# The second MLP layer of a hybrid decoder layer: eight units by seven products, with two running sets of PSUM banks

## The chip, the cores and the metric

The kernel runs on one core of one Trainium2 chip. A core has five engines with queues of their own: PE (TensorE, the matmuls), DVE (VectorE), ACT (ScalarE), POOL (GpSimd) and SP (SyncE, which here issues the transfers). Data lies in HBM, in SBUF and, for what PE writes, in the eight banks of PSUM, each 128 rows of 512 fp32 numbers. The metric is the device time of one execution in microseconds (us); lower is better.

## The reference

One Hymba layer in fp32: 1024 positions of width 1024, an attention and a recurrence side by side, an output projection, and an MLP of width 4096.

```python
x = x + rmsnorm(mixed, mix_post_norm[layer])
h = rmsnorm(x, mlp_pre_norm[layer])
ff = jnp.square(jax.nn.relu(h @ w_ff1[layer])) @ w_ff2[layer]
x = x + rmsnorm(ff, mlp_post_norm[layer])
```

The change lies in the third line's second product (1024 x 4096 by 4096 x 1024) and in the fourth line. The norm divides a row by its root mean square and multiplies by a gain per column.

## The kernel before

**Precision.** Every fp32 operand is split into a high part (ACT copies it in a rounded format) and a low part (DVE subtracts), in `split_into` (L97, L98), and each product is three matmuls, high by high, high by low and low by high, in `three_pass` (L101 to L103) and in the first layer's `mm1` (L1489 to L1491). Names end in h or l accordingly: ah and al are the activations' parts, bh and bl the weights'.

**First layer.** The 4096 hidden columns are 16 pairs of 256. A pair (`ff1(q)`, q = 2 to 15; pairs 0 and 1 go together ahead of them) is computed by the seven products of the Strassen-Winograd scheme, each of 12 matmuls, and the results are combined, passed through the squared ReLU and summed into the seven left operands which the second layer's seven products need: `act_sums` on POOL, L1557 to L1560. `act_store` writes them to `act_dram`. Two pairs make one unit of 512 hidden columns of the second layer, so there are units 0 to 7. Pairs 0 and 1, unit 0, are only squared and stored as they are (`act_plain`, into `act_raw`).

**Second layer.** It is a sum over the eight units. Units 1 to 7 go by seven products each, in three groups, (1), (2, 3, 4) and (5, 6, 7). Within a group the order is product, then unit, so that a product of all the group's units adds up in the same four banks (one for each block of 128 rows), and is then collected:

```python
if g == 0:
    ...
    S.activation(acc_at(p, i), pm, AF.Copy)
elif g == NG - 1 and p == 4:
    V.tensor_tensor(out=acc_at(p, i), in0=acc_at(p, i), in1=pm, op=ALU.subtract)
else:
    V.tensor_tensor(out=acc_at(p, i), in0=pm, in1=acc_at(p, i), op=ALU.add)
```

There is one SBUF sum for each of the seven products. The four output quadrants are made of them by `fold_in` (L1916) in the last group and after. One product of one unit is 24 matmuls (4 row blocks, 2 halves of 128 hidden rows, 3 passes). Unit 0 is computed last, in full: for each of the eight row blocks of the output 24 matmuls into two banks `fe`, whose content is added to the quadrants (L2053); ACT squares the sums with a running total (L2054), POOL makes the row's factor (L2058, L2066, L2067), DVE multiplies by the gain (`norm_gain`, L2028) and adds the residual (`end_out`, L2023), and two transfers of 256 KB write the row block. The last block's second half is cut in two (L2044 to L2048), with DVE squaring one of them.

**What sets the order.** Nothing is scheduled by a planner: the engines run their instructions in the order in which the program is written. At unit-product n the program issues the load of the left operand of n + 3 (`a_load`, L1824), prepares the parts of n + 2 (`prep`), makes the weights' sum for n + 4 (`prep_sum`, `b_source`, L1849 and L1855, on DVE), loads weights as buffers come free (`b_pump`, L1830), then issues the matmuls and, where the product is complete, its collection. Work beside these has its place in the table `at_last` or in `start2`, which runs between the products of the first layer's last pair. SBUF buffers come from pools (`small`, `large`) and are handed on when `drop` was called; a buffer's next writer waits for its last reader.

Of the kernel before, what the change touches and what calls it, by code (L numbers as in the profile page):

```python
# [35 lines left out]
def hymba_layer(ctx, tc, x, w_in, w_out, w_ff1, w_ff2, g_pre, lb_logits, g_mix, g_post,  # L36
# [63 lines left out]
    def three_pass(dst, lhs, rhs, start, stop):  # L100
        TE.matmul(dst, lhs[0], rhs[0], start=start, stop=False)  # L101
        TE.matmul(dst, lhs[0], rhs[1], start=False, stop=False)  # L102
        TE.matmul(dst, lhs[1], rhs[0], start=False, stop=stop)  # L103
# [1320 lines left out]
    act_raw = dp.tile([P, 2, 2, 2, 512], F32, name="actr")  # L1424
    act_dram = {u: dp.tile([P, 7, 2, 512], F32, name=f"actd{u}") for u in range(1, NPAIR // 2)}
# [145 lines left out]
    def act_plain(q):  # L1571

        l = lay.pop(q)
        nc.sync.dma_start(out=act_raw[:, q, 0, 0], in_=l["E1"][:, 0])
        nc.sync.dma_start(out=act_raw[:, q, 0, 1], in_=l["X"][:, 0])
        nc.sync.dma_start(out=act_raw[:, q, 1], in_=l["E1"][:, 1:3])
        drop(l["E1"], l["X"])


# [224 lines left out]
    for q in range(2, NPAIR - 1):  # L1804
        ff1(q)

# [3 lines left out]
    GROUPS = ((1,), (2, 3, 4), (5, 6, 7))  # L1810
    NG = len(GROUPS)
    APLACE = {1: 0, 2: 1, 4: 2, 5: 3, 6: 4, 7: 5, 3: 6}
    ORDER = (1, 5, 7, 6, 2, 4, 3)
    LAST = (1, 5, 7, 6, 2, 3, 4)
    units = [(g, p, h) for g in range(NG) for p in (LAST if g == NG - 1 else ORDER) for h in range(len(GROUPS[g]))]
# [4 lines left out]
    def a_load(n):  # L1820
        if n < n_units:
            g, p, h = units[n]
            axraw[n] = small.get(f"ar{n}")
            nc.sync.dma_start(out=axraw[n], in_=act_dram[GROUPS[g][h]][:, APLACE[p]])  # L1824

# [8 lines left out]
    def b_pump(g):  # L1834

        spare = sum((g, h) not in tt for h in range((len(GROUPS[g]) + 1) // 2)) if g >= 0 else 0
        while b_queue and b_queue[0][0] <= g + 1 and len(large.free) > spare:
            b_load(*b_queue.pop(0))

# [3 lines left out]
    def b_source(g, p, h):  # L1843
# [4 lines left out]
        if p == 7:  # L1848
            V.tensor_tensor(out=b12, in0=b22, in1=b12, op=ALU.subtract)  # L1849
            return b12  # L1850
        if p == 5 and h % 2 == 0:
            tt[g, h // 2] = large.get(f"tt{g}{h}")
        t = tt[g, h // 2][:, 2 * (h % 2):2 * (h % 2) + 2]
        in0, in1 = {5: (b12, b11), 6: (b22, t), 4: (t, b21)}[p]
        V.tensor_tensor(out=t, in0=in0, in1=in1, op=ALU.subtract)  # L1855
        return t
# [3 lines left out]
    def prep_sum(n):  # L1860
        if n < n_units:
            g, p, h = units[n]
            bsrc[n] = b_source(g, p, h)
            if g == NG - 1 and p == 4:
                drop(braw.pop((g, h, 1)))

    def prep(n):
# [9 lines left out]
        order = LAST if g == NG - 1 else ORDER  # L1877
        done_p = order[:order.index(p) + 1]

        def now(*needs):  # L1880
            return p in needs and all(x in done_p for x in needs)

        if p == 4 and (h % 2 or h == len(GROUPS[g]) - 1):
            drop(tt[g, h // 2])
        if now(1, 5, 7):
            drop(braw.pop((g, h, 0)))
        if now(2, 3, 4, 6, 7) and g < NG - 1:
            drop(braw.pop((g, h, 1)))

    cur = []  # L1890

    def mm2(n, i, first, last):
        (ah, al), (bh, bl) = aop[n], bop[n]
        c = slice(i * P, (i + 1) * P)
        for j in range(2):
            three_pass(cur[i], (ah[:, j, c], al[:, j, c]), (bh[:, j], bl[:, j]), first and j == 0, last and j == 1)

    def acc_at(p, i):
        return acc[p][i // 2][:, i % 2]

    def collect(g, p, i):

        pm = cur[i]
        if g == 0:
            if i == 0:
                acc[p] = [small.get(f"acc{p}{j}") for j in range(2)]
            S.activation(acc_at(p, i), pm, AF.Copy)
        elif g == NG - 1 and p == 4:
            V.tensor_tensor(out=acc_at(p, i), in0=acc_at(p, i), in1=pm, op=ALU.subtract)
        else:  # L1910
            V.tensor_tensor(out=acc_at(p, i), in0=pm, in1=acc_at(p, i), op=ALU.add)  # L1911
        drop(pm)

    def fold_in(p, o, j, op=ALU.add):

        V.tensor_tensor(out=acc[p][j], in0=acc[o][j], in1=acc[p][j], op=op)  # L1916


    def start2(p):
# [5 lines left out]
        elif p == 5:  # L1925
            drop(*bops["T1"])
            prep(0)
            prep_sum(2)
        elif p == 6:
# [4 lines left out]
            prep_sum(3)  # L1934
        elif p == 4:
            drop(*bops["T4"])
        elif p == 7:
            drop(*bops["T3"])
            prep(2)
# [18 lines left out]
    def plain_load(kind, q):  # L1958
        t = praw[kind, q] = large.get(f"{kind}p{q}")
        if kind == "w":  # L1960
            src = w_ff2[2 * q * P:(2 * q + 2) * P].rearrange("(j p) c -> p j c", j=2)
        else:
            src = act_raw[:, q].rearrange("p j a c -> p j (a c)")
        nc.sync.dma_start(out=t.rearrange("p (j a) c -> p j (a c)", j=2), in_=src)

    def plain_split(kind, q, j):
        if j == 0:
            plain[kind, q] = [large.get(f"{kind}p{x}{q}", F32R) for x in "hl"]
        hi, lo = (x[:, 2 * j:2 * j + 2] for x in plain[kind, q])
        split_into(hi, lo, praw[kind, q][:, 2 * j:2 * j + 2])  # L1970
        if j == 1:
            drop(praw.pop((kind, q)))

    def plain_op(kind, q, j, c0, n):
        return tuple(x.rearrange("p (j a) c -> p j (a c)", j=2)[:, j, c0:c0 + n] for x in plain[kind, q])

    n_last = n_units - 7 * len(GROUPS[-1])
# [162 lines left out]
```

## Time and profile before

| | us |
|---|---|
| median of 3 runs | 1231.04 (1230.53 to 1233.12) |
| the profiled execution | 1229.69 |
| its span in the trace | 1227.9 |
| busy: PE / DVE / ACT / POOL | 1206.1 / 840.0 / 538.8 / 289.7 |
| granted TensorE clock, mean | 0.997 of full speed |
| second layer, first matmul to the end of the span | 910.08 to 1227.9 |

The span is what the profile covers; the profiled execution took 1.79 us more than it. Rows of the trace give the start and duration of an instruction, its line, engine and operation, the tile that it writes and those that it reads, their shapes, and in brackets the idle time before it with the work that ended the wait. In groups, xcount is followed by the busy time in us, the mean of one in ns, and the idle time before them with its releasers.

### The profile page before, as it was taken

Reading aid. Unit: us, or ns where it says so; the run is one execution under the profiler, and the core shown is the slowest. Engines: PE = TensorE matmul, PEld = TensorE weight load, DVE = VectorE, ACT = ScalarE, POOL = GpSimd, SP = SyncE. Lnnn points to the kernel's source line nnn. Section 1 sums busy time; section 2 is a strip of 40 time slices with the busy share of each in tenths; the row PEclk is TensorE's granted clock in tenths of the full one; section 3 lists DMA queues with packets and bytes.
Section 4 is the critical chain, followed back from the end, with each engine's and each line's share of the span. In section 5 each row is a group of like instructions: output and inputs, shape, how many; then the busy total and the mean of one; then the engine's idle time right before and its main releaser. Section 6 shows DMA issues by size and latency. Waiting matters only on the chain. (4 is left out here: it accounts for less than half of the span.)

```text
span 1227.9 us, 16736 instructions
## 1 busy us (share of the span) xinstructions
PE 1206.1 (98%) x6264; PEld 1026.4 (84%) x6264; DVE 840.0 (68%) x1329; ACT 538.8 (44%) x1058; POOL 289.7 (24%) x253
## 2 busy tenths in 40 slices
PE   8999999999999999999999999999999999999997
PEld 8898989888788887778888888888878888888886
DVE  5584858575565657665589566666675866698966
ACT  7633333332566567844664222222247434344312
POOL 0000000032303130154230786565530000000012
PEclk9999999999999999999999999999999999999999
DMA  5221312123443455353424554353668444434423
GB/s 215 66 73 52 87 52 70 35 69 104 107 113 100 115 144 180 103 174 121 173 76 154 181 180 151 133 189 129 222 262 315 145 153 137 154 104 132 176 70 120
DMA packets 80417, 163.77 MB, mean 133 GB/s; under 512 B 23632, under 2 KB 30544, under 8 KB 80080
## 3 DMA queue, kind: packets, MB, share of 16 engines
q1 hardware_dynamic: 80336, 162.70, 40.5%
q8 instruction: 49, 0.80, 0.3%
q14 instruction: 32, 0.26, 0.1%
HBM read 112.16 MB, written 46.19 MB: 129 GB/s over the span
## 5 line engine op out<-in xcount | busy, mean ns | idle before, releaser
L101 PE MATMUL f<-bh,ah 128*128 128x512 f32 x392 | 152.5, 389 | 0.0
L102 PE MATMUL f<-bl,ah 128*128 128x512 f32 x392 | 152.5, 389 | 0.0
L103 PE MATMUL f<-bh,al 128*128 128x512 f32 x392 | 152.5, 389 | 0.0
L98 DVE TENSOR_TENSOR al<-ar,ah 128x1024 fp32r<-128x1024 f32 x49 | 60.6, 1237 | 48.2 <-ACT ah L97 17.7
L101 PEld LDWEIGHTS f<-bh,ah 128*128 128x128 f32 x392 | 73.6, 188 | 15.4
L102 PEld LDWEIGHTS f<-bl,ah 128*128 128x128 f32 x392 | 73.6, 188 | 15.2
L103 PEld LDWEIGHTS f<-bh,al 128*128 128x128 f32 x392 | 73.6, 188 | 15.2
L97 ACT ACTIVATE ah<-ar 128x1024 fp32r<-128x1024 f32 x49 | 52.2, 1065 | 51.1 <-PE f L103 25.4
L2058 POOL TENSOR_SCALAR fp<-fss 128x1 f32<-128x1 f32 x8 | 3.7, 459 | 269.5 <-ACT fd L2054 269.5
L862 DVE TENSOR_TENSOR pt<-pt,pt 128x512 fp32r<-128x512 f32 (+1 forms) x56 | 34.9, 630 | 34.1 <-ACT pt L861 33.9
L1557 POOL TENSOR_TENSOR e<-x,e 128x512 f32<-128x512 f32 x14 | 20.6, 1475 | 135.8 <-DVE x L1508 135.8
L93 POOL TENSOR_SCALAR ms<-hss 128x8 f32<-128x8 f32 x4 | 1.0, 258 | 214.9 <-ACT ysq L600 214.9
L821 ACT ACTIVATE prob<-prob,unm 128x128 f32<-128x128 f32 (+2 forms) x96 | 48.5, 508 | 4.7 <-DVE unm L815 4.3
L97 ACT ACTIVATE bh<-br 128x1024 fp32r<-128x1024 f32 x28 | 29.9, 1066 | 42.9 <-PE f L103 37.6
L663 POOL TENSOR_TENSOR ql<-qf,q 64x512 fp32r<-64x512 f32 x16 | 21.5, 1346 | 97.3 <-ACT q L662 96.7
L861 ACT ACTIVATE pt<-pt 128x512 fp32r<-128x512 f32 (+1 forms) x56 | 30.3, 549 | 24.0 <-PE pt L858 23.6
L1911 DVE TENSOR_TENSOR acc<-f,acc 128x512 f32<-128x512 f32 x52 | 33.8, 685 | 8.2 <-PE f L103 8.2
L97 ACT ACTIVATE bh<-tt 128x1024 fp32r<-128x1024 f32 x21 | 22.3, 1061 | 38.2 <-PE f L103 25.9
L763 DVE CUSTOM_DVE_ANT_0 prob<-ps,tab 128x256 f32<-128x256 f32 (+3 forms) x56 | 26.5, 502 | 17.3 <-PE ps L760 11.0
L98 DVE TENSOR_TENSOR bl<-br,bh 128x1024 fp32r<-128x1024 f32 x28 | 34.2, 1221 | 2.9 <-PE f L102 2.5
L98 DVE TENSOR_TENSOR wl<-raw,wh 128x1024 fp32r<-128x1024 f32 x21 | 26.9, 1279 | 9.5 <-ACT wh L97 9.1
L879 PE MATMUL pov<-pt,v 128*128 128x512 f32 (+3 forms) x144 | 30.4, 320 | 0.3 <-DVE pt L862 0.2
(1650 smaller groups left out, 3806.4 us busy)
## 6 DMA issues: line engine op xcount, KB each, us to landing
ar<-actd SPq DMA_DIRECT2D x49, 512.0 KB, 3.7
raw<-in_w_in_dram SPq DMA_DIRECT2D x28, 512.0 KB, 3.6
w1r<-in_w_ff_dram SPq DMA_DIRECT2D x14, 1024.0 KB, 6.4
br<-in_w_ff_dram SPq DMA_DIRECT2D x14, 1024.0 KB, 8.0
actd<-e SPq DMA_DIRECT2D x17, 768.0 KB, 4.3
actd<-e SPq DMA_DIRECT2D x11, 1024.0 KB, 4.1
xr<-in_x_dram SPq DMA_DIRECT2D x8, 512.0 KB, 9.7
raw<-in_w_out_dram SPq DMA_DIRECT2D x8, 512.0 KB, 3.9
```

The lines of the kernel that those rows point to most:

```text
L97: S.activation(hi, src, AF.Copy)
L98: eng.tensor_tensor(out=lo, in0=src, in1=f32(hi), op=ALU.subtract)
L101: TE.matmul(dst, lhs[0], rhs[0], start=start, stop=False)
L102: TE.matmul(dst, lhs[0], rhs[1], start=False, stop=False)
L103: TE.matmul(dst, lhs[1], rhs[0], start=False, stop=stop)
L663: G.tensor_tensor(out=lo[a:b], in0=full[a:b], in1=f32(stacks[i]["q"][a:b, sl]), op=ALU.subtract)
L763: V.tensor_tensor_reduce(out=out, in0=pS, in1=tab, scale=1.0, scalar=-3.0e38, op0=ALU.add, op1=ALU.max, accum_out=acc)
L821: S.activation(pe, pe, AF.Exp, bias=r["nm"][:, j:j + 1], accum_out=r["dn"][:, j:j + 1])
L861: S.activation(hi, ptv, AF.Copy)
L862: V.tensor_tensor(out=lo, in0=ptv, in1=f32(hi), op=ALU.subtract)
L879: TE.matmul(o, v.rearrange("p a d -> p (a d)"), x[q], start=g == 0 and q == 0, stop=g == 2 + hf and n == len(ops) - 1 and q == 1, skip_gro ...
L1911: V.tensor_tensor(out=acc_at(p, i), in0=pm, in1=acc_at(p, i), op=ALU.add)
```

## The change

Unit 0 joins the others. The groups are (0, 1), (2, 3, 4) and (5, 6, 7), all by seven products: 56 unit-products in place of 49 and the plain unit. For that, unit 0's left operands are made as well: `act_plain` stores the four plain pieces of pairs 0 and 1, `act_again` reads a pair's 1 MB back after pairs 5 and 8 of the first layer, `act_rest` makes the three sums with four operations on DVE ahead of pairs 7 and 10, and stores them.

The seven SBUF sums become four, one for each quadrant (C11, C12, C21, C22), and what several quadrants share is added up in PSUM. Three sets of banks take turns. Set x holds products 1 and 2: product 1 is copied by ACT to set y, and product 2 is then added onto it in x, which gives C11. On y, products 6, 7 and 4 are added one after another, and what is there is collected after each: for C12, C22 and C21. Set z (in x's banks) holds product 5, then 3, collected for C22 and C12. The weights' sums take other signs and another order.

In the last group, after products 7 and 5, DVE also adds the earlier groups' C21 and C12 into the banks. So the last products end whole output rows in PSUM: `end_row` squares a bank on ACT, makes the factor and multiplies by the gain from the bank, `send_row` adds the residual and writes the row block. `ready_piece` does the squares and gains of C11 and C22 beforehand. Rows 4 to 7 end along the first unit of product 3, rows 0 to 3 along its second and third, whose matmuls are interleaved by row block, 12 for each row. Three sums and splits that stood between the products of the first layer's last pair stand at the first unit of the second layer now, and weights are loaded one piece at every second unit.

```diff
     def act_plain(q):
 
         l = lay.pop(q)
-        nc.sync.dma_start(out=act_raw[:, q, 0, 0], in_=l["E1"][:, 0])
-        nc.sync.dma_start(out=act_raw[:, q, 0, 1], in_=l["X"][:, 0])
-        nc.sync.dma_start(out=act_raw[:, q, 1], in_=l["E1"][:, 1:3])
+        nc.sync.dma_start(out=act_dram[0][:, 0:3, q], in_=l["E1"][:, 0:3])
+        nc.sync.dma_start(out=act_dram[0][:, 3, q], in_=l["X"][:, 0])
         drop(l["E1"], l["X"])
 
+    def act_again(q):
+        again[q] = large.get(f"e1{q}x")
+        nc.sync.dma_start(out=again[q], in_=act_dram[0][:, 0:4, q])
+
+    def act_rest(q, eng=V):
+        e = again.pop(q)
+        a11, a12, a22, a21 = (e[:, i] for i in range(4))
+        eng.tensor_tensor(out=a22, in0=a21, in1=a22, op=ALU.add)
+        eng.tensor_tensor(out=a21, in0=a11, in1=a21, op=ALU.subtract)
+        eng.tensor_tensor(out=a11, in0=a22, in1=a11, op=ALU.subtract)
+        eng.tensor_tensor(out=a12, in0=a12, in1=a11, op=ALU.subtract)
+        nc.sync.dma_start(out=act_dram[0][:, 3:7, q], in_=e)
+        drop(e)
...
     for q in range(2, NPAIR - 1):
+        if q in (7, 10):
+            act_rest((q - 7) // 3)
         ff1(q)
+        if q in (5, 8):
+            act_again((q - 5) // 3)
...
-    GROUPS = ((1,), (2, 3, 4), (5, 6, 7))
+    GROUPS = ((0, 1), (2, 3, 4), (5, 6, 7))
...
-    ORDER = (1, 5, 7, 6, 2, 4, 3)
-    LAST = (1, 5, 7, 6, 2, 3, 4)
+    ORDERS = ((1, 2, 6, 5, 7, 3, 4), (1, 6, 2, 7, 5, 4, 3), (1, 6, 2, 7, 5, 4, 3))
...
         t = tt[g, h // 2][:, 2 * (h % 2):2 * (h % 2) + 2]
-        in0, in1 = {5: (b12, b11), 6: (b22, t), 4: (t, b21)}[p]
-        V.tensor_tensor(out=t, in0=in0, in1=in1, op=ALU.subtract)
-        return t
+        dst, in0, in1, op = {6: (t, b12, b11, ALU.add), 5: (b11, b22, t, ALU.subtract),
+                             4: (t, b21, t, ALU.subtract)}[p]
+        V.tensor_tensor(out=dst, in0=in0, in1=in1, op=op)
+        return dst
...
+    sums, begun = {}, set()
+    ROLE = {1: "x", 2: "x", 6: "y", 7: "y", 4: "y", 5: "z", 3: "z"}
...
     def collect(g, p, i):
 
-        pm = cur[i]
...
+        pm = sums[ROLE[p]][i]
+        if p == 1:
+            S.activation(sums["y"][i], pm, AF.Copy)
+            return
+        final = g == NG - 1
+        if not (final and p in (3, 4)):
+            o = {2: 11, 6: 12, 7: 22, 5: 22, 4: 21, 3: 12}[p]
+            if o not in acc:
+                acc[o] = [small.get(f"acc{o}{j}") for j in range(2)]
+            if (o, i) not in begun:
+                begun.add((o, i))
+                S.activation(acc_at(o, i), pm, AF.Copy)
+            else:
+                V.tensor_tensor(out=acc_at(o, i), in0=pm, in1=acc_at(o, i), op=ALU.add)
+            if final and p in (7, 5):
+                V.tensor_tensor(out=pm, in0=pm, in1=acc_at({7: 21, 5: 12}[p], i), op=ALU.add)
+            if p in (2, 4, 3):
+                drop(pm)
...
+    def ready_piece(t):
+
+        o, j = (11, 0) if t < 4 else (22, 1)
+        c, ss = acc_at(o, t % 4), col(f"fss{t}")
+        S.activation(half(f"fd{t}"), c, AF.Square, accum_out=ss)
+        G.tensor_scalar(fpart[:, t:t + 1], ss, 1.0 / D, EPS, op0=ALU.mult, op1=ALU.add)
+        V.tensor_tensor(out=c, in0=c, in1=gend[:, j], op=ALU.mult)
+
+    def end_row(t, last=False):
+        role, o, j = ("z", 12, 1) if t < 4 else ("y", 21, 0)
+        pm, c, ss, rf, ms = sums[role][t % 4], acc_at(o, t % 4), col(f"fst{t}"), col("frf"), col("fms")
+        S.activation(half(f"fe{t}"), pm, AF.Square, accum_out=ss)
+        (V if last else G).tensor_scalar(ms, ss, 1.0 / D, fpart[:, t:t + 1], op0=ALU.mult, op1=ALU.add)
+        G.tensor_tensor(out=rf, in0=ms, in1=nhalf[:, :1], op=ALU.pow)
+        V.tensor_tensor(out=c, in0=pm, in1=gend[:, j], op=ALU.mult)
+        drop(pm)
+        scale2[t] = rf
+
+    def send_row(t):
+
+        xr, rf = x2r.pop(t), scale2.pop(t)
+        for o, j in ((11, 0), (12, 1)) if t < 4 else ((22, 1), (21, 0)):
+            c = acc_at(o, t % 4)
+            V.scalar_tensor_tensor(c, c, rf, xr[:, j], op0=ALU.mult, op1=ALU.add)
+            nc.sync.dma_start(out=rows_of(out, t)[:, j * 512:(j + 1) * 512], in_=c)
+        drop(xr)
...
+        elif h == 0:
+            for i in range(4):
+                mm2(n, i, False, False)
+                end_row(4 + i)
+                if i:
+                    send_row(3 + i)
+            send_row(7)
+        elif h == 1:
+            for i in range(4):
+                mm2(n, i, False, False)
+                mm2(n + 1, i, False, True)
+                end_row(i, i == 3)
+                if i:
+                    send_row(i - 1)
+            send_row(3)
```

Three places show how the order moves. On DVE, at the head of pair 7 of the first layer (x and wd7 are tiles of pairs 6 and 7, e10x is the piece that is read back). Before:

```order
L1508 SCALAR_TENSOR_TENSOR e_6997<-e_6997 128x512 x2
L1543 TENSOR_TENSOR x_6998<-f16c,x_6998 128x512
L1508 SCALAR_TENSOR_TENSOR x_6998<-x_6998 128x512
L98 TENSOR_TENSOR wd7l<-w1r_6887,wd7h 128x1024
L1524 TENSOR_TENSOR x_7130<-f17d,x_7130 128x512
```

and now:

```order
L1507 SCALAR_TENSOR_TENSOR x_6998<-x_6998 128x512
L1586 TENSOR_TENSOR e10x<-e10x 128x512
L1587 TENSOR_TENSOR e10x<-e10x 128x512
L1588 TENSOR_TENSOR e10x<-e10x 128x512
L1589 TENSOR_TENSOR e10x<-e10x 128x512
L98 TENSOR_TENSOR wd7l<-w1r_6885,wd7h 128x1024
L1523 TENSOR_TENSOR x_7135<-f17d,x_7135 128x512
```

The four operations of `act_rest` stand between pair 6's last and pair 7's first. On ACT, in the last group of the changed kernel, the four copies of product 1 from set x (f) to set y (f22y), with the splits around them:

```order
L97 ACTIVATE ah_9753<-ar_9714 128x1024
L97 ACTIVATE bh_9757<-tt_9643 128x1024
L1921 ACTIVATE f22y_9761<-f_9686 128x512
L1921 ACTIVATE f22y_9762<-f_9687 128x512
L1921 ACTIVATE f22y_9763<-f_9688 128x512
L1921 ACTIVATE f22y_9764<-f_9689 128x512
L97 ACTIVATE ah_9795<-ar_9751 128x1024
L97 ACTIVATE bh_9799<-tt_9724 128x1024
```

Before, no copy of this kind was there. The bh ahead of them belongs to product 6, whose matmuls add onto set y. On DVE, the end of the program (acc_8605 and acc_8473 are the last row's halves before). Before:

```order
L2028 TENSOR_TENSOR acc_8605<-acc_8605,gend 128x512
L2044 TENSOR_TENSOR acc_8473<-fe_10617,acc_8473 128x256
L2046 TENSOR_TENSOR acc_8473<-fe_10617,acc_8473 128x256
L2048 ISA fd_10630,fmore<-acc_8473 128x256
L2048 ISA fmore 128x1
L2050 TENSOR_SCALAR fmore<-fmore,fp_10611 128x1
L2066 TENSOR_SCALAR fms<-fss_10593,fmore 128x1
L2028 TENSOR_TENSOR acc_8473<-acc_8473,gend 128x512
L2023 SCALAR_TENSOR_TENSOR acc_8605<-acc_8605,frf,x2r_10452 128x512
L2023 SCALAR_TENSOR_TENSOR acc_8473<-acc_8473,frf,x2r_10452 128x512
```

and now:

```order
L1993 TENSOR_TENSOR acc_8582<-f_10142,gend 128x512
L2002 SCALAR_TENSOR_TENSOR acc_8505<-acc_8505,frf,x2r_10395 128x512
L2002 SCALAR_TENSOR_TENSOR acc_8581<-acc_8581,frf,x2r_10395 128x512
L1991 TENSOR_SCALAR fms<-fst_10553,fpart 128x1
L1993 TENSOR_TENSOR acc_8582<-f_10143,gend 128x512
L2002 SCALAR_TENSOR_TENSOR acc_8506<-acc_8506,frf,x2r_10397 128x512
L2002 SCALAR_TENSOR_TENSOR acc_8582<-acc_8582,frf,x2r_10397 128x512
L2002 SCALAR_TENSOR_TENSOR acc_8506<-acc_8506,frf,x2r_10399 128x512
L2002 SCALAR_TENSOR_TENSOR acc_8582<-acc_8582,frf,x2r_10399 128x512
```

Fewer operations stand between the last product and the factor's cue (fms), and the output operations of row 2 (x2r_10397) now stand behind it, ahead of those of row 3.

186 lines of the change are left out of this document (55 added, 131 removed).

## The prediction

> **What bounds the kernel now.** I read the page's head, busy line and chain of waits first, then the windows of the second layer, then what PE waited for there.
>
> ```profile
> span 1227.9 us, 16736 instructions
> ...
> PE 1206.1 (98%) x6264; PEld 1026.4 (84%) x6264; DVE 840.0 (68%) x1329; ACT 538.8 (44%) x1058; POOL 289.7 (24%) x253
> ...
> PE 45%; DVE 1%; issue 0%; ACT 0%; POOLq 0%; DVEq 0%; ACTq 0%
> ```
>
> The chain is shown for less than half of the span, and almost all that is shown is PE. The windows (us, then busy time and count of PE, PEld, DVE, ACT, POOL, then granted clock, DMA share, GB/s) say it for the stage that changes, from 910 us to the end:
>
> ```profile
> 900.00:1000.00 100.00, 100.00 (x442) 82.53 (x441) 72.71 (x70) 51.87 (x65) 6.07 (x4) 1.00 0.68 242
> 1000.00:1100.00 100.00, 100.00 (x443) 82.81 (x442) 73.96 (x75) 40.29 (x39) 0.00 (x0) 1.00 0.40 127
> 1100.00:1200.00 100.00, 100.00 (x443) 82.79 (x442) 81.00 (x89) 35.11 (x45) 5.51 (x10) 1.00 0.38 127
> 1200.00:1228.00 28.00, 20.32 (x90) 16.50 (x88) 18.92 (x32) 5.71 (x18) 7.64 (x13) 0.94 0.28 110
> ```
>
> PE has no idle time in 300 us, at full clock; DVE has 19 to 27 in each 100, ACT 48 and more, the DMA engines a third and more. Of the waits from 880 us on, only one is PE's:
>
> ```profile
> PE f115a L1489 <- ACT x L1511: 0.7, 1, 0.7
> ```
>
> So in this stage a matmul less is time less, and work on another engine is free until it makes PE wait.
>
> **The matmuls.** One unit in one product is 4 row blocks by 2 halves by 3 passes = 24 matmuls. Before: 7 units x 7 products x 24 = 1176, and unit 0 in full, 8 rows x 24 = 192: 1368. After: 8 x 7 x 24 = 1344. That is 24 fewer, and PE's list of instructions is shorter by as many. What is one worth?
>
> ```profile
> L101 PE MATMUL f<-bh,ah 128*128 128x512 f32 x392 | 152.5, 389 | 0.0
> ...
> L101 PE MATMUL fe<-wph,aph 128*128 128x512 f32 x64 | 24.9, 389 | 0.0
> ```
>
> and the first and the last of them in the timeline (start, us):
>
> ```profile
> 910.08 0.39 PE L101 MATMUL f<-bh,ah 128*128 128x512 f32 x1
> ...
> 1219.93 0.39 PE L103 MATMUL fe<-wph,apl 128*128 128x512 f32 x1
> ```
>
> Not the 389 ns of the groups: that is one matmul from start to end, and they overlap. From the first to the last start there are 1367 steps in 1219.93 - 910.08 = 309.85 us, 0.2267 us each. 24 x 0.2267 = **5.44 us** removed. (24 x 0.389 = 9.3 would be the misreading.)
>
> **What feeds PE there.** These rows price the new work:
>
> ```profile
> L98 DVE TENSOR_TENSOR al<-ar,ah 128x1024 fp32r<-128x1024 f32 x47 | 58.2, 1238 | 48.2 <-ACT ah L97 17.7 <-issue 16.3 <-PE f L102 14.1
> L97 ACT ACTIVATE ah<-ar 128x1024 fp32r<-128x1024 f32 x46 | 49.0, 1066 | 48.5 <-PE f L103 25.4 <-DMA ar<-actd 13.8 <-DVE al L98 6.5
> L1911 DVE TENSOR_TENSOR acc<-f,acc 128x512 f32<-128x512 f32 x52 | 33.8, 685 | 8.2 <-PE f L103 8.2
> ...
> L1916 DVE TENSOR_TENSOR acc<-acc,acc 128x1024 f32<-128x1024 f32 x14 | 17.1, 1219 | 0.1
> L1907 ACT ACTIVATE acc<-f 128x512 f32<-128x512 f32 x28 | 15.4, 630 | 10.6 <-PE f L103 10.6
> ...
> L2053 DVE TENSOR_TENSOR acc<-fe,acc 128x512 f32<-128x512 f32 x15 | 10.4, 691 | 9.4 <-PE fe L103 9.3
> ```
>
> and from the waits, ACT's longest kind (in total, times, longest):
>
> ```profile
> ACT bh L97 <- PE f L103: 63.6, 25, 3.3
> ```
>
> DVE: seven more unit-products are 14 splits of 1.24 (+17.4), four more sums of weights at the 1.22 of an all-SBUF operation of that size (+4.9); away go 8 splits of the plain unit (-9.8), the 14 folds (-17.1) and the additions of plain results (-10.4). Collections into SBUF are 8, 24 and 16 by group, with 8 additions into banks 56, as many as the 52 + 4 before. In sum about -15 us: free. ACT: 14 splits more, 8 fewer, 28 copies as before (16 collections, 12 seeds of a bank set): +6.4 us on an engine that is half idle. SP's queue: seven loads of 512 KB and two of 1 MB more, four of 1 MB fewer, on DMA engines that are 0.68 busy at most. Sums over a stage don't exclude a late one, so I went through the new dependencies unit by unit (5.44 us each).
>
> *Seeds.* In the last two groups product 6 follows product 1 and adds onto ACT's copy of it. A bank's six matmuls take 1.36 us, so bank i is complete 4.08 us before product 6 reaches its copy. A copy from PSUM to PSUM is not in the trace; by its SBUF relative it takes 0.63, by a split twice its width 1.07, either way inside 4.08. What matters is what stands ahead of it in ACT's queue: a bh split, the kind that waits for PE up to 3.3 us. There it is one whose buffers come free with the end of a unit two units earlier. Cost 0, up to 3.4 us of lateness free.
>
> *Additions into a bank* (last group, after products 7 and 5). Four collections and four additions, 8 x 0.685 = 5.5 us, then the splits of one unit, 2 x 1.24 = 2.5: done 8.0 us after the product's end, while PE needs them two units, 10.9 us, after it. Spare 2.9. An operation that both reads and writes PSUM is not in the trace; between 0.685 and twice that, where the spare just lasts (4 x 0.685 = 2.7), it costs 0. I take 0.685, the nearest form.
>
> *Banks.* A new set always takes banks collected one product before, 10.9 or 16.3 us: 0.
>
> **Pairs 7 and 10 of the first layer.** Here the change adds four additions on DVE at the head of the pair. The first two rows below are DVE's, the gap of 2.88 us in the second is where they go; behind them wait the low half of wd7 and the addition that empties f17d, which PE needs at 748.37. POOL works at the same time (second fence); the third is PE's first matmul that needs f17d:
>
> ```profile
> 738.42 0.69 DVE L1508 SCALAR_TENSOR_TENSOR x<-x 128x512 f32<-128x512 f32 x1
> 741.99 2.20 DVE L98 TENSOR_TENSOR wd7l<-w1r,wd7h 128x1024 fp32r<-128x1024 f32 x1 [2.88 <-ACT wd7h L97]
> 744.11 0.68 DVE L1524 TENSOR_TENSOR x<-f17d,x 128x512 f32<-128x512 f32 x1
> 744.71 1.18 DVE L98 TENSOR_TENSOR wf<-s,wf 128x512 fp32r<-128x512 f32 x1
> ...
> 899.76 0.68 DVE L98 TENSOR_TENSOR wf<-s,wf 128x512 fp32r<-128x512 f32 x1
> ```
>
> ```profile
> 739.19 1.28 POOL L1557 TENSOR_TENSOR e<-x,e 128x512 f32<-128x512 f32 x1 [3.24 <-DVE x L1508]
> ...
> 743.06 2.28 POOL L1560 TENSOR_TENSOR e<-e,e 128x512 f32<-128x512 f32 x1
> ```
>
> ```profile
> 748.37 0.39 PE L1489 MATMUL f17d<-T40h,wd7h 128*128 128x512 f32 x1
> ```
>
> Alone, such an operation takes 0.68 (899.76), four 2.72: they fit the gap. But beside POOL the same form took 1.18, the wide one 2.20 against 1.24, and POOL's 2.28 against 1.28: an encounter costs each side 0.5 to 1.0. With one each, the four take 2.72 + 4 x (0.5 to 1.0) = 4.7 to 6.7, so 1.8 to 3.8 us late; PE's need at 748.37 is 3.58 after the end of x<-f17d (744.11 + 0.68 = 744.79). Stall 0 to 0.2 a pair. If each loses a whole POOL operation, 4 x (0.68 + 1.28) = 7.84, late 4.96, stall 1.4. I take 0.1 a pair, 0.2 in all (pair 10 runs the same code), ends 0 and 2.8. The Trainium skill, SBUF — State Buffer, section "Who interferes with whom", says that a DVE operation with two SBUF inputs and a GpSimd one that reads SBUF exclude each other, and the second to issue blocks until the first has finished; the 2.20 beside 1.24 agrees in kind, and by that rule the upper end, 2.8, would stand.
>
> The reloads and stores of these pieces are SP's, and their readers come two pairs, or a stage, later: 0.
>
> **The end.** The last matmul ends at 1219.93 + 0.39 = 1220.32; the span ends 7.58 us later. The last row of each helper there, and the output transfers (count, size, median us to landing):
>
> ```profile
> 1222.05 0.21 DVE L2066 TENSOR_SCALAR fms<-fss,fmore 128x1 f32<-128x1 f32 x1
> 1222.18 0.68 DVE L2028 TENSOR_TENSOR acc<-acc,gend 128x512 f32<-128x512 f32 x1
> 1223.30 1.42 DVE L2023 SCALAR_TENSOR_TENSOR acc<-acc,frf,x2r 128x512 f32<-128x512 f32 x2 [0.44 <-POOL frf L2067]
> ```
>
> ```profile
> 1222.41 0.86 POOL L2067 TENSOR_TENSOR frf<-fms,nhalf 128x1 f32<-128x1 f32 x1 [2.71 <-DVE fms L2066]
> ```
>
> ```profile
> 1218.42 0.63 ACT L2054 ACTIVATE fd<-acc 128x512 f32<-128x512 f32 x1 [1.97 <-DVE acc L2053]
> 1218.96 0.19 ACT L2054 ACTIVATION_READ_ACCUMULATOR fd<-acc 128x1 f32 x1
> ```
>
> ```profile
> out_dram<-acc SPq DMA_DIRECT2D x16, 256.0 KB, 2.0
> ```
>
> Before, the last two output operations start 2.98 us after the last matmul. After: ACT squares a bank in place of an SBUF tile, taken alike, 0.63 + 0.19 = 0.82; DVE's fms 0.21, POOL's power 0.86: ready at about 2.1 with the hand-overs. But DVE has, behind fms, the gain of row 3 (0.69) and the two output operations of row 2 (1.42) to do first: 1.03 + 0.2 + 2.1 = 3.3 us. So +0.3, and four output transfers of 256 KB instead of two follow within 3 us. Ends: -0.9 (were row 2 out before), +1.0 (half of a 2.0 transfer queued). I take **+0.3**. In the 16.3 us before, DVE has 7 gains and 12 output operations, 7 x 0.69 + 6 x 1.42 = 13.4, and keeps up.
>
> **The sum** against the profiled execution: 1227.9 - 5.44 + 0.2 + 0.3 = 1222.96 of span; with the 1.79 around it (1229.69 - 1227.9) 1224.75. The median of the runs shown, 1231.04, is 1.35 above the profiled execution: 1231.04 - 4.94 = **1226.1**.
>
> **The rivals.**
>
> 1. *POOL and DVE hold each other up at pairs 7 and 10.* For it: 2.20, 1.18 and 2.28 above, in the very place. Against it: 3.58 us of spare before PE, and that only one operation of several lost. At its upper end 1226.1 - 0.2 + 2.8 = **1228.7**, which cannot be told from before.
>
> 2. *The end is longer*: row 2's outputs and row 3's cue together and the transfers queue; +1.0 more: **1227.1**, still faster. For it: DVE's order; against it: the DMA share of 0.28 there.
>
> 3. *Slower: the additions into banks.* Nothing prices an operation with PSUM on both sides. From 1.4 us on, the split of the unit two ahead is late, twice (after products 7 and 5). At 2.5 us, two passes of a wide operation, 4 x (2.5 - 0.685) - 2.9 = 4.4 us at each: 1226.1 + 8.7 = **1234.8**; the gain is gone from 2.0 us on, where it is 2 x (5.3 - 2.9) = 4.8. For it: DVE is the busiest helper, 81.00 of the last full 100, and works in order. Against it: the mixed form, PSUM in and SBUF out, is 0.685, all-SBUF of this size 0.68, so neither side of an operation shows a price of its own.
>
> That the change doesn't shorten PE's list is excluded by the list itself.
>
> **How the numbers follow.** Forecast 0.66, rival 1 0.14, rival 2 0.12, rival 3 0.08. The measurement tells about 0.2%, 2.46 us, from no change: faster is below 1228.58, slower above 1233.5. Forecast and 0.10 of rival 2, with 0.02 of rival 1, are faster: 0.78. Most of rival 1 (0.12) and 0.02 of rival 2 are the same: 0.14. Rival 3: 0.08. Range: below, without the two costs (-0.5), with the shorter end (-1.2 from the one taken) and the spread of the runs shown (0.5, less what is counted twice) some 1223.8; above, rival 1's 1228.7 with a longer end, 1230. I give 1223.7 to 1230.0.
>
> **What would show it.** Right: PE 100.00 busy in every 100 us from 910 to the end, the last matmul some 5.2 us earlier, no wait of PE above 1 us after pair 6. Rival 1: a PE wait for DVE's x or wd7l in pair 7 (near 748) and pair 10, with the four additions taking over 1.5 us each. Rival 2: more than 8.5 us from the last matmul to the end. Rival 3: PE waiting for DVE's al or bl twice in the last 60 us, additions into banks above 1.4 us. A wait of PE for ACT's seed copies behind product 1 would refute the working on the seeds. A pitch other than 0.2267 would refute the whole sum.

## The result, and the profile after

| | before | after |
|---|---|---|
| median, us | 1231.14 (1230.53 to 1233.26) | 1225.45 (1222.76 to 1227.67) |
| ratio, 95% interval | | 0.9949 (0.9931 to 0.9966) |
| profiled execution / its span | 1229.69 / 1227.9 | 1225.18 / 1223.4 |
| first matmul of the second layer | 910.08 | 911.04 |
| first to last start there | 309.85 (1368 matmuls) | 304.41 (1344) |
| end of the last matmul to the end of the span | 7.58 | 7.56 |

The change gains 0.5%. Forecast were 1226.1 and a gain of 4.94; the medians are 5.7 apart. In a second set of runs the changed kernel's median was 1223.53 beside 1230.67 before, ratio 0.9946 (0.9934 to 0.9958).

The first and the last matmul of the second layer, in the timeline of the changed kernel:

```profile
911.04 0.39 PE L101 MATMUL f<-bh,ah 128*128 128x512 f32 x1
...
1215.45 0.39 PE L103 MATMUL f<-bh,al 128*128 128x512 f32 x1
```

1343 steps in 304.41 us are 0.2267 each, the pitch of before to the last digit. The stage is 309.85 - 304.41 = 5.44 us shorter, the product of 24 and that pitch. Behind it the same 7.6 us. The two profiled spans differ by 4.5 and not by 5.44, because the stage starts 0.96 later. That is no cost of the change: from 523 to 614 us PE takes 1.55 longer, where its clock drops for longer in this execution (last section); ahead of that it is 0.33 earlier, and the first layer's last pair, from which the change took three sums and splits, is 0.25 shorter (20.02 us for 20.27; that this is the reason was not tested).

The windows of the stage, as before it:

```profile
900.00:1000.00 100.00, 100.00 (x443) 82.81 (x442) 74.61 (x69) 47.79 (x58) 8.83 (x4) 1.00 0.67 237
1000.00:1100.00 100.00, 100.00 (x443) 82.81 (x442) 66.15 (x67) 40.95 (x43) 0.00 (x0) 1.00 0.45 141
1100.00:1200.00 100.00, 100.00 (x443) 82.81 (x442) 76.06 (x82) 44.31 (x61) 6.27 (x14) 1.00 0.36 111
```

PE is still busy throughout. DVE (the third pair of numbers) has 66 and 76 where it had 74 and 81. Over the whole stage it is busy 224.7 us where it was 236.6, 11.9 less (the sum said some 15), and ACT 133.8 where it was 129.0 (+4.9; the sum said 6.4). Neither is worth anything while PE doesn't wait. PE's waits from 700 us on are the one of before:

```profile
PE f115a L1488 <- ACT x L1510: 0.7, 1, 0.7
```

Pair 7 of the first layer, DVE above and POOL below:

```profile
740.24 0.69 DVE L1586 TENSOR_TENSOR e10x<-e10x 128x512 f32<-128x512 f32 x1
740.96 1.67 DVE L1587 TENSOR_TENSOR e10x<-e10x 128x512 f32<-128x512 f32 x1
742.65 1.67 DVE L1588 TENSOR_TENSOR e10x<-e10x 128x512 f32<-128x512 f32 x1
744.36 1.67 DVE L1589 TENSOR_TENSOR e10x<-e10x 128x512 f32<-128x512 f32 x1
745.95 2.31 DVE L98 TENSOR_TENSOR wd7l<-w1r,wd7h 128x1024 fp32r<-128x1024 f32 x1
748.18 0.68 DVE L1523 TENSOR_TENSOR x<-f17d,x 128x512 f32<-128x512 f32 x1
```

```profile
740.40 1.68 POOL L1556 TENSOR_TENSOR e<-x,e 128x512 f32<-128x512 f32 x1 [3.26 <-DVE x L1507]
742.15 1.62 POOL L1557 TENSOR_TENSOR e<-e 128x512 f32<-128x512 f32 x1
743.74 1.74 POOL L1558 TENSOR_TENSOR e<-e,x 128x512 f32<-128x512 f32 x1
```

The two engines take turns: an operation of 0.68 alone (899.76 before the change) takes 1.67 on DVE, and POOL's of 1.28 takes 1.62 to 1.74. The four additions last 5.8 us (740.24 to 746.03), and x<-f17d ends at 748.86. PE's f17d<-T40h starts at 749.58, right behind its predecessor. Of 3.58 us of spare 0.72 are left. In pair 10 the four additions take the same 0.68, 1.67, 1.67 and 1.66, and 0.73 are left.

The forms that the trace of before lacked, in the groups of the second layer, a copy from bank to bank and an addition into a bank:

```profile
L1934 DVE TENSOR_TENSOR f22y<-f22y,acc 128x512 f32<-128x512 f32 x4 | 2.8, 688 | 0.0
...
L1921 ACT ACTIVATE f22y<-f 128x512 f32<-128x512 f32 x4 | 2.3, 582 | 8.0 <-PE f L103 8.0
```

The last additions behind product 7, and the splits that follow them:

```profile
1166.92 0.69 DVE L1932 TENSOR_TENSOR acc<-f22y,acc 128x512 f32<-128x512 f32 x1
1167.53 0.69 DVE L1934 TENSOR_TENSOR f22y<-f22y,acc 128x512 f32<-128x512 f32 x1
1168.12 1.22 DVE L98 TENSOR_TENSOR al<-ar,ah 128x1024 fp32r<-128x1024 f32 x1
1169.26 1.22 DVE L98 TENSOR_TENSOR bl<-br,bh 128x1024 fp32r<-128x1024 f32 x1
```

The end, on DVE:

```profile
1214.55 1.41 DVE L2002 SCALAR_TENSOR_TENSOR acc<-acc,frf,x2r 128x512 f32<-128x512 f32 x2
1216.73 0.21 DVE L1991 TENSOR_SCALAR fms<-fst,fpart 128x1 f32<-128x1 f32 x1 [0.78 <-ACT fe L1990]
1216.86 0.68 DVE L1993 TENSOR_TENSOR acc<-f,gend 128x512 f32<-128x512 f32 x1
1217.46 2.73 DVE L2002 SCALAR_TENSOR_TENSOR acc<-acc,frf,x2r 128x512 f32<-128x512 f32 x4
```

The x4 of the last row are row 2's two output operations and then row 3's. DVE stands idle for 0.78 us ahead of fms while row 2's could have run, and is the last to finish, at 1220.19, 4.35 us after the last matmul (before: 4.40).

### The profile page after: what moved, and what is told of

The parts are those of the page before. It is cut to its first block, busy times and chain, and to the rows that moved or that the text cites. A ratio compares the mean times of both kernels' runs of the same rounds, so it can differ in the third digit from the quotient of the medians.

```text
span 1223.4 us, 16690 instructions
## 1 busy us (share of the span) xinstructions
PE 1202.6 (98%) x6240; PEld 1023.8 (84%) x6240; DVE 836.9 (68%) x1313; ACT 541.9 (44%) x1064; POOL 298.5 (24%) x253
## 5 line engine op out<-in xcount | busy, mean ns | idle before, releaser
L101 PE MATMUL f<-bh,ah 128*128 128x512 f32 x256 | 99.6, 389 | 0.0
L102 PE MATMUL f<-bl,ah 128*128 128x512 f32 x256 | 99.6, 389 | 0.0
L103 PE MATMUL f<-bh,al 128*128 128x512 f32 x256 | 99.6, 389 | 0.0
L97 ACT ACTIVATE bh<-br 128x1024 fp32r<-128x1024 f32 x40 | 42.2, 1055 | 62.8 <-PE f L102 24.0
L102 PEld LDWEIGHTS f<-bl,ah 128*128 128x128 f32 x256 | 48.0, 188 | 10.1
L101 PEld LDWEIGHTS f<-bh,ah 128*128 128x128 f32 x256 | 48.0, 188 | 9.9
L103 PEld LDWEIGHTS f<-bh,al 128*128 128x128 f32 x256 | 48.0, 188 | 9.9
L98 DVE TENSOR_TENSOR bl<-br,bh 128x1024 fp32r<-128x1024 f32 x40 | 49.9, 1247 | 4.8 <-PE f22y L102 2.6
L1932 DVE TENSOR_TENSOR acc<-f,acc 128x512 f32<-128x512 f32 x24 | 16.6, 692 | 24.4 <-PE f L103 24.2
L376 ACT ACTIVATE inat<-pig,rstd 128x128 f32<-128x128 f32 x24 | 8.7, 364 | 46.4 <-PE pig L103 46.4
```

The lines of the kernel that those rows point to most:

```text
L97: S.activation(hi, src, AF.Copy)
L98: eng.tensor_tensor(out=lo, in0=src, in1=f32(hi), op=ALU.subtract)
L101: TE.matmul(dst, lhs[0], rhs[0], start=start, stop=False, **kw)
L102: TE.matmul(dst, lhs[0], rhs[1], start=False, stop=False, **kw)
L103: TE.matmul(dst, lhs[1], rhs[0], start=False, stop=stop, **kw)
```

## The experiments

### Is the gain the 24 matmuls?

```diff
+            if n == 0:
+                for i in range(4):
+                    mm2(n, i, True, False)
             for i in range(4):
                 mm2(n, i, open_, shut)
```

> The changed kernel, with the 24 matmuls of the first unit-product of the second layer issued twice (the second set starts the banks anew, so nothing that is computed changes). Theory: the gain is the 24 matmuls and nothing else. Then first to last matmul of the second layer goes from 304.4 to 304.4 + 24 x 0.2267 = 309.8 us, and the median from 1225.45 to 1230.9, no difference from before (ratio 1.000, within 0.002). Rival, part of the gain has another source (fewer operations on DVE, another end): below 1229.5. Rival, a matmul is worth its 389 ns: 1234.8.

Measured: 1230.74 beside 1230.71 before, ratio 1.0001 (0.9991 to 1.0011).

```profile
911.62 0.39 PE L101 MATMUL f<-bh,ah 128*128 128x512 f32 x1
...
1221.47 0.39 PE L103 MATMUL f<-bh,al 128*128 128x512 f32 x1
```

309.85 us from the first to the last start (expected were 309.8), the figure of before. With the 24 matmuls back the whole gain is gone: everything else in the change, new feeding, new banks, new end, sums to nothing that the interval, some 1.2 us to either side, could show.

### How near are the four additions of pairs 7 and 10 to PE's path?

```diff
         eng.tensor_tensor(out=a12, in0=a12, in1=a11, op=ALU.subtract)
+        for x in (a22, a21, a11, a12):
+            eng.tensor_tensor(out=x, in0=x, in1=x, op=ALU.max)
```

> The changed kernel, with eight operations on DVE ahead of pairs 7 and 10 in place of four (the four added ones take the maximum of a tile with itself, so nothing that is computed changes). In the changed kernel the four took 0.69 + 3 x 1.67 us beside POOL, and the addition that empties f17d ended 0.72 us before PE needed it. Theory: that spare of 0.72 is all there is, and each added operation costs 0.7 (if POOL is past) to 1.67 (if not): PE waits 4 x 0.7 - 0.72 = 2.1 to 4 x 1.67 - 0.72 = 6.0 us in each pair, 4 to 12 us in all, 1229.5 to 1237.5, nearer the upper end since POOL goes straight on to the next pair's sums. Rival, the place is not near the path: no wait of PE in pairs 7 and 10, 1225.5.

Measured: 1240.81, 15.4 us above the changed kernel's 1225.45 and beyond what either theory gave. PE's waits:

```profile
PE f110d L1488 <- DVE x L1523: 6.0, 1, 6.0
PE f17d L1488 <- DVE x L1523: 6.0, 1, 6.0
```

DVE's four added operations, and PE after the wait:

```profile
746.10 6.82 DVE L1591 TENSOR_TENSOR e10x<-e10x 128x512 f32<-128x512 f32 x4
```

```profile
755.86 0.77 PE L1488 MATMUL f17d<-T40h,wd7h 128*128 128x512 f32 x1 [5.97 <-DVE x L1523]
756.43 0.63 PE L1489 MATMUL f17d<-T40l,wd7h 128*128 128x512 f32 x1
...
758.99 0.49 PE L1489 MATMUL f17d<-T41l,wd7h 128*128 128x512 f32 x1
```

The waits are the upper end of the theory, 4 x 1.67 - 0.72 = 6.0 in each pair: the place is on the path as soon as the 0.72 is used up, and every further operation there costs its price with POOL beside it. The rest is what the theory left out. The second layer starts at 926.73 here, 15.69 us later than in the changed kernel, and 0.15 of that lie ahead of pair 7: 15.54 - 2 x 5.97 = 3.60, 1.8 a pair. After the idle time of 6 us the clock is lower, 0.58 in the window behind it, and seven matmuls (756.43 to 758.99) start 0.43 apart, where 0.2267 is the pitch:

```profile
755.00:760.00 5.00, 4.14 (x12) 3.34 (x13) 4.62 (x7) 2.49 (x3) 0.00 (x0) 0.58 1.03 381
```

The Trainium skill, TensorE: Matmul & The Clock Gate, section "Part 1: The HAM clock gate", gives half the clock after an idle window of about 3.4 us; the trace agrees: a pitch of 0.43 is about half speed, and it lasts some 3 us. In these traces a shorter wait can be enough: near 520 us the clock falls after one of 2.85 us (last section).

### How late may the seeds be?

```diff
         if p == 1:
+            for k in range((0, 5, 10)[g] if i == 0 else 0):
+                S.activation(half(f"dm{g}{k}"), pm, AF.Copy)
             S.activation(sums["y"][i], pm, AF.Copy)
             return
```

> The changed kernel, with ACT held up by copies of product 1's first bank into a scratch tile, just ahead of the four seed copies: 5 of them in the second group, 10 in the third. Theory: the seeds have some 3.3 us of spare (the first ends at 1114.46, PE starts on its bank at 1117.8). At 0.5 to 0.6 us a copy, 5 of them (2.5 to 3.0) cost nothing, and 10 (5.0 to 6.0) make PE wait 1.7 to 2.7 us once, in the third group: 1227 to 1228. Rival, the seeds stand on the path: a wait in both groups, 2.5 to 3 and 5 to 6 us, 1233 or more.

Measured: 1226.01, a single run within the spread of the changed kernel's own; the waits decide. PE waited in the third group only:

```profile
PE f22y L101 <- ACT f22y L1923: 1.5, 1, 1.5
```

```profile
1112.85 5.00 ACT L1922 ACTIVATE dm<-f 128x512 f32<-128x512 f32 x10 [5.71 <-PE f L103]
1117.64 2.17 ACT L1923 ACTIVATE f22y<-f 128x512 f32<-128x512 f32 x4
```

The ten copies put the first seed off by 1117.64 - 1112.85 = 4.8 us, and PE waited 1.5 of them: a spare of 3.3, as the theory had it. Five copies, 2.4 us by the same pitch, cost nothing in the second group. The stage took 306.22 us, 1.81 longer, 0.3 more than the wait.

### How much more can DVE add into the banks?

```diff
             if final and p in (7, 5):
-                V.tensor_tensor(out=pm, in0=pm, in1=acc_at({7: 21, 5: 12}[p], i), op=ALU.add)
+                for op in (ALU.add, ALU.subtract, ALU.add):
+                    V.tensor_tensor(out=pm, in0=pm, in1=acc_at({7: 21, 5: 12}[p], i), op=op)
```

> The changed kernel, with each of the eight additions into a bank of the last group done three times (add, subtract, add). The prediction gave a product's collections and additions 5.5 us behind the product's end and so a spare of 2.9: by that working 8 more of 0.69 us after product 7 and after product 5 make PE wait 5.5 - 2.9 = 2.6 us each time, 1225.45 + 5.2 = 1230.7, with waits of PE for the low half al or bl near 1178 and 1194. By the trace of the changed kernel the additions run bank by bank along the product's last unit, and only 1.3 us of them lie behind its end: then 16 operations at 0.61 from 1162.8 and one unit's splits (2.3) end near 1175, before 1177.8, and nothing changes: 1225.5.

Measured: 1227.38, a single run, and one wait of PE, 2.5 us, after product 5; none after product 7. The stage took 307.24 us, 2.83 longer. Neither theory: the first gave 2.6 twice, the second nothing.

```profile
PE f22y L102 <- DVE bl L98: 2.5, 1, 2.5
```

```profile
1170.80 2.16 DVE L1935 TENSOR_TENSOR f22y<-f22y,acc 128x512 f32<-128x512 f32 x3
1172.87 1.22 DVE L98 TENSOR_TENSOR al<-ar,ah 128x1024 fp32r<-128x1024 f32 x1
...
1182.02 1.22 DVE L98 TENSOR_TENSOR bl<-tt,bh 128x1024 fp32r<-128x1024 f32 x1
1183.15 0.68 DVE L1932 TENSOR_TENSOR acc<-f,acc 128x512 f32<-128x512 f32 x1
...
1191.74 2.16 DVE L1935 TENSOR_TENSOR f<-f,acc 128x512 f32<-128x512 f32 x3
...
1194.94 1.22 DVE L98 TENSOR_TENSOR bl<-tt,bh 128x1024 fp32r<-128x1024 f32 x1
```

After product 7 the spare holds, as the second theory said. But DVE has no idle time left from there. In the changed kernel the first collection of product 5 starts at 1179.16, here at 1183.15; counted from the first matmul of the stage (911.04 and 910.41) that is 4.6 us late. The eight operations added after product 5 put off the splits behind them by another 5.4, and with a spare of 7.3 (below) the sum is 4.6 + 5.4 - 7.3 = 2.7, about the wait measured: the debt of the first place comes due at the second. The spare is one account over the last group, not one for each place: of 16 added operations, 16 x 0.69 = 11 us, all but 2.5 were absorbed.

### The end: what it is made of

The changed kernel itself ran beside three versions of its end.

> The changed kernel once more, beside the kernels that change its end. Theory: 24 matmuls less, 5.44 us, and an end as long as before (7.56 against 7.58 us): ratio to before 0.9956, 1225.3 where before is 1230.7. A run is longer where its granted clock is lower (0.997, 0.996, 0.993), in this kernel as in the kernel before.

Measured: 1223.53, 1.8 less than expected, ratio 0.9946 (0.9934 to 0.9958, which still holds the expected 0.9956). The stage takes 304.41 us and the end 7.56, as in its other profile; the stage starts 1.6 earlier (909.44). The clocks go with the times only loosely here: 1223.58 at 0.995, and 1224.93 at 0.996.

**Rows sent earlier.**

```diff
                 mm2(n + 1, i, False, True)
-                end_row(i, i == 3)
                 if i:
                     send_row(i - 1)
+                end_row(i, i == 3)
             send_row(3)
```

> The changed kernel, with each of rows 0 to 2 sent (its two output operations on DVE and its two transfers) ahead of the next row's square and gain, no longer behind them. Theory: the end is as long as it is because DVE does row 2's two output operations (1.4 us) between the last factor and row 3's. Out of the way, row 3's start when POOL's power is there, at 1217.6 in place of 1218.8, and the last ends at 1219.0 in place of 1220.2: 1.2 us less, and up to 0.7 more where four transfers no longer queue (2.7 us to landing against 2.0 before). 1.2 to 1.9 us below the changed kernel. Rival, the end is set by the transfers alone, whatever DVE does: no difference.

Measured: last matmul 1214.74, end of the span 1221.1: 6.36 us, 1.20 less. Median 1222.93, ratio 0.9941 (0.9929 to 0.9952); beside the changed kernel's 1223.53 the medians' difference, 0.6, is within the runs' spread, and the end in the trace carries the verdict.

```profile
1213.91 1.42 DVE L2002 SCALAR_TENSOR_TENSOR acc<-acc,frf,x2r 128x512 f32<-128x512 f32 x2 [0.31 <-POOL frf L1992]
1215.63 0.21 DVE L1991 TENSOR_SCALAR fms<-fst,fpart 128x1 f32<-128x1 f32 x1 [0.30 <-ACT fe L1990]
1215.76 0.68 DVE L1993 TENSOR_TENSOR acc<-f,gend 128x512 f32<-128x512 f32 x1
1216.58 1.41 DVE L2002 SCALAR_TENSOR_TENSOR acc<-acc,frf,x2r 128x512 f32<-128x512 f32 x2
```

Row 2 goes out ahead of fms, and only row 3's two operations follow the gain: the last ends at 1217.99, 3.25 us after the last matmul in place of 4.35. DVE's part is 1.10 of the 1.20; of the 0.7 us that the transfers might have added, 0.10 came.

**The last two units one after the other.**

```diff
             for i in range(4):
                 mm2(n, i, False, False)
+            for i in range(4):
                 mm2(n + 1, i, False, True)
                 end_row(i, i == 3)
```

> The changed kernel, with the last two units of product 3 one after the other: rows 0 to 3 end in the last unit, one every 1.36 us, in place of one every 2.72. Theory: DVE needs 1.95 us a row (a gain and two output operations), more than 1.36 and less than 2.72; three rows' backlog lets the last output operation end 1.1 us later, and the transfers, closer together, add up to 0.7: 1.1 to 1.8 us more than the changed kernel, with the last matmul at the same place. Rival, the end is bound by the last row's own chain: no difference.

Measured: last matmul 1214.77, end 1223.4: 8.63 us, 1.07 more. Median 1226.53, ratio 0.9970 (0.9956 to 0.9984). The last output operation ends 5.39 us after the last matmul in place of 4.35: the backlog on DVE is as worked out, and the transfers added nothing to it. The medians are 3.0 apart, of three and six runs; of the 1.6 between the two profiled executions (1225.2 and 1223.58) the end is 1.07, and the start of the stage, 909.97 against 909.44, the rest.

**Rows ended from SBUF.**

```diff
-        if not (final and p in (3, 4)):
+        if True:
...
-            if final and p in (7, 5):
-                V.tensor_tensor(out=pm, in0=pm, in1=acc_at({7: 21, 5: 12}[p], i), op=ALU.add)
...
-        pm, c, ss, rf, ms = sums[role][t % 4], acc_at(o, t % 4), ...
+        c = acc_at(o, t % 4)
+        pm, c, ss, rf, ms = c, c, ...
...
                 mm2(n + 1, i, False, True)
+                collect(g, p, i)
                 end_row(i, i == 3)
...
-        if shut:
+        if shut and not (final and p == 3):
             for i in range(4):
                 collect(g, p, i)
```

> The changed kernel without the eight additions into banks: products 4 and 3 are collected into the sums of C21 and C12 as in the other groups, and a row is squared and scaled from SBUF. Theory: an addition of 0.69 us now stands between the last matmul and the last row's square, nothing else lies on the path: 0.7 us more than the changed kernel, all of it behind the last matmul. Rival, DVE's share of the last 16 us, 13.4 us of work before, 16.2 with the additions, becomes the bound: 2 us more or above, and rows late from product 3 on.

Measured: last matmul 1214.00, end 1225.7: 11.7 us, 4.1 more than the changed kernel's end. Median 1229.57, ratio 0.9995 (0.9979 to 1.0011). What the rival forecast came: rows are late, and by more than 2 us.

```profile
1205.65 2.73 DVE L2000 SCALAR_TENSOR_TENSOR acc<-acc,frf,x2r 128x512 f32<-128x512 f32 x4
1208.30 0.68 DVE L1932 TENSOR_TENSOR acc<-f,acc 128x512 f32<-128x512 f32 x1
...
1213.95 0.68 DVE L1932 TENSOR_TENSOR acc<-f,acc 128x512 f32<-128x512 f32 x1
1215.47 0.69 DVE L1992 TENSOR_TENSOR acc<-acc,gend 128x512 f32<-128x512 f32 x1 [0.85 <-ACT fe L1989]
1216.08 1.41 DVE L2000 SCALAR_TENSOR_TENSOR acc<-acc,frf,x2r 128x512 f32<-128x512 f32 x2
1217.41 0.68 DVE L1932 TENSOR_TENSOR acc<-f,acc 128x512 f32<-128x512 f32 x1
...
1219.74 2.73 DVE L2000 SCALAR_TENSOR_TENSOR acc<-acc,frf,x2r 128x512 f32<-128x512 f32 x4
```

Row 3's addition starts 3.4 us after the last matmul's end, where 0.1 would do. Two things make that up. DVE is behind before row 0: it ends the output operations of rows 6 and 7 only at 1208.3, and row 0's addition starts 2.5 us after row 0's last matmul, row 1's still 1.9. From there on DVE takes 1217.41 - 1213.95 = 3.46 us from one addition to the next: four operations and an idle 0.85, since the gain stands behind the square, and the square now behind DVE's own addition. A row comes every 2.72, so two rows add 2 x 0.74 = 1.5. Without the idle time a row would take 2.61 and the backlog would shrink: the first part is DVE's load, as the rival had it, the second the hand-over to ACT and back within each row.

The median is 6.0 above the changed kernel's, more than the 4.1 of the end; the longer of the six runs have granted clocks down to 0.991, and the profiled one, 1227.47, was the second shortest.

**The last transfer in halves**, on the reordered end.

```diff
+            w = 256 if t == 3 and j else 512
+            for s in range(0, 512, w):
...
```

> The reordered end (each of rows 0 to 2 sent ahead of the next row's square and gain), and the last output operation of row 3 cut in two halves of 256 columns, each with its own transfer of 128 KB. From the last matmul to the end of the span the reordered end took 6.36 us, of which 3.23 lie behind the start of the last transfer's data. Theory, a transfer's time grows with its size: the last one is half as long, 0.1 to 0.4 us less, 6.0 to 6.3. Rival, the time of a small transfer is fixed, and one more has to be issued: 6.36 or up to 0.3 more. By the runs so far the median should be 1.2 to 1.6 us below the changed kernel's, 1222 to 1224, and the ratio to before about 0.9940.

Measured: last matmul 1215.88, end 1222.3: 6.42 us, 0.06 more; median 1224.25, ratio 0.9953 (0.9937 to 0.9969), a little above the 1222 to 1224 that was expected. Median us to landing, over the 256 KB and the 128 KB transfers, and then, of the reordered end, over the 256 KB transfers of its last 16 us alone:

```profile
out_dram<-acc SPq DMA_DIRECT2D x15, 256.0 KB, 2.7
...
out_dram<-acc SPq DMA_DIRECT2D x2, 128.0 KB, 1.9
```

```profile
out_dram<-acc SPq DMA_DIRECT2D x12, 256.0 KB, 2.1
```

The 2.7 holds earlier output transfers too. Beside the 2.1 of the last ones a half lands only some 0.2 sooner, and the last half is issued later: 3.51 us after the last matmul, where the last whole transfer was issued after 3.28, since DVE and SP each have one operation more to do first. From that issue to the end of the span it is 2.91 us in place of 3.08. What the smaller size saves, the second issue costs, and the rival holds.

## Why the prediction was right

*The matmuls.* 5.44 us forecast, 5.44 measured in the stage, and all of them lost again when 24 matmuls were put back. The pitch from first to last start was the right price; 389 ns would have given 9.3.

*Seeds.* Cost 0 and 3.4 us of spare were given; the copies from PSUM to PSUM took 0.58, and five copies' lateness was free while ten's cost 1.5.

*Additions into a bank.* Cost 0 and the price, 0.685 by the nearest form (0.69 measured), were right. The spare was mis-sized. The step "then the splits of one unit, 2 x 1.24 = 2.5: done 8.0 us after the product's end" put all eight operations behind the product. They run along its last unit, bank by bank; the last bank's collection starts at 1166.92 and the splits end at 1170.48, 3.6 us later, so the spare is 10.9 - 3.6 = 7.3 and not 2.9. And the step treated the two places apart, while the debt of one is carried to the other. Rival 3's point of 1.4 us an operation was too low: with three operations in the place of one, 2.1 us, PE waited once.

*Pairs 7 and 10.* The four additions were given 4.7 to 6.7 us and PE a wait of 0 to 0.2; they took 5.8, and PE didn't wait. "An encounter costs each side 0.5 to 1.0" was right at its upper end for the three DVE operations that met POOL (0.99 each); POOL's lost 0.3 to 0.5. The rule that the prediction cites from the Trainium skill would have had each wait for a whole POOL operation, 1.96; measured is 1.67, with POOL's own at some 1.7 in place of 1.28. Rival 1's mechanism is there, and its sign of over 1.5 us an addition came for three of the four; its wait of PE did not. One more operation at 1.67 would have used up the 0.72; with four more the wait came in full.

*The end.* +0.3 forecast, -0.02 measured. The order of DVE's work was read rightly: rows 2 and 3 stood behind fms, and with row 2 out of the way the end was 1.2 us shorter (the prediction's bound: 0.9). The term was too long by a step that added up durations, 1.03 + 0.2 + 2.1 = 3.3: operations in a row start sooner than the one ahead has ended, by the starts above 1216.73, 1216.86, 1217.46, and row 3's output begins some 3.0 after the last matmul. The transfers, for which a part of the 0.3 was meant, added nothing. That DVE "keeps up" in the last 16 us held, but only because the rows end in PSUM. The prediction priced the additions into banks as a cost of nothing, and not what they save: without them the end is 4.1 us longer. By the traces 5.44 - 4.1 = 1.3 us of the gain would be left, too little for the runs to tell from nothing (ratio 0.9995, 0.9979 to 1.0011).

*The total.* 1226.1 forecast, 1225.45 and 1223.53 measured in two sets. The end's 0.3 and the pairs' 0.2 were not spent; what remains lies ahead of the stage, where the start of the second layer varies (below), and in no term. So the 5.44 and the missing waits were foreseen; that the total came within 0.7 in the first set is in part luck, and the second set's 1223.53 lies just below the 1223.7 at which the range ends. The sign of a last matmul some 5.2 us earlier came as 4.5 in one profile and 6.1 in the other, for the same reason.

## What to carry to other kernels

Where one engine is busy without a gap, price a removed instruction by the pitch from first to last, and then spend the effort on each new operation's neighbours: what spare does the waiting engine have at that place, and is it shared with the next place? Read an engine's queue for what stands ahead of the last critical step; here two output operations that were ready 0.8 us earlier cost 1.2 us at the end. And an addition that an engine can make ahead of time into the accumulator can be worth more than its own duration, when it takes work out of that engine's fullest stretch and a hand-over between two engines out of a chain that repeats for each row.

## What was not expected of the hardware

DVE and POOL, each with operations on SBUF tiles of 128x512, slow each other in a steady alternation: 0.68 becomes 1.67 and 1.28 becomes 1.62 to 1.74, so that the starts of both are about 1.7 us apart. Together they take less than one after the other: undisturbed, in the kernel before, DVE's starts are 0.60 apart at the least and POOL's 1.25, in sum 1.85 (by durations, 0.68 + 1.28 = 1.96).

A wait of PE costs more than the length that the profile gives for it: 0.3 us on top of 1.5 (306.22 - 304.41 = 1.81) and of 2.5 (307.24 - 304.41 = 2.83), and 1.8 on top of 6.0. Half of the 0.3 is only the way of counting: idle time begins where the matmul before it ends, 0.39 after its start, while in a stream the next would have started after 0.2267, 0.16 sooner. Another 0.1 is the first step behind the wait, 0.33 long. The clock stays at 1.00 there; behind the 6.0 it doesn't.

The time of one kernel varies by some 5 us between executions, in the changed kernel from 1222.76 at a granted clock of 0.997 to 1227.67 at 0.993, in the kernel before from 1228.38 at 0.998 to 1233.16 at 0.993. In the profiles the difference lies ahead of the second layer, whose start varies from 909.19 to 911.62 (the run with eight operations in pairs 7 and 10 apart), while its length is 304.41 or 304.42 in every version with 1344 matmuls and no added wait. One place is the wait near 520 us, where PE's clock drops; the changed kernel's window there, then that of the kernel before:

```profile
520.00:530.00 10.00, 7.15 (x24) 5.68 (x23) 3.98 (x9) 2.89 (x5) 2.28 (x2) 0.68 0.93 311
```

```profile
520.00:530.00 10.00, 7.15 (x33) 5.78 (x33) 5.21 (x10) 3.10 (x6) 2.28 (x2) 0.83 0.93 300
```

A clock of 0.68 and of 0.83, with the same idle time of 2.85 us, and 24 matmuls against 33. In windows of 2 us the changed kernel has 0.50 from 524 to 530, the kernel before only from 526 to 528. The eleven profiles bear out that this makes executions differ. From the first matmul behind that wait (pz) to the first of pair 2 (f12a) PE takes 89.9 to 90.0 us in the three whose window reads 0.83 (the kernel before, the additions three times, the rows from SBUF), and 90.9 to 91.6 in the eight with 0.66 to 0.69. From f12a to the second layer the changed kernel and its versions take 296.45 to 296.49, where no wait was added. So this place is worth 0.9 to 1.7 us from one execution to another. The rest lies ahead of it, where pz starts between 522.00 and 524.02, and its cause stays open, as does what sets the length of the drop.
